# Token-shift mixing by token groups, each stored alone, and a shorter head before the mixing phase of a two-layer streaming trunk

## The chip, the cores and the metric

One core of a Trainium2 chip runs the whole program. Times are device microseconds (us) of one execution. The engines of the core run their own queues in the order fixed at build time: TensorE (PE in the profile, its weight loads PEld), VectorE (DVE), ScalarE (ACT), GpSimd (POOL) and SyncE (SP, which issues nearly all DMAs here). An instruction waits on semaphores for what other engines or transfers must have done.

## What is computed

Two layers of a streaming encoder. In each, one projection `w_in` of the normalised input feeds three parallel groups of heads: a short gated convolution, latent attention (MLA), and RWKV-7 time mixing. The time mixing works on columns that are first mixed with those of the token ahead. Cut to this part, the reference is:

```
h = rmsnorm(x, norm_g)
z = h @ w_in
xin, bg, cg, ga, cq, ckv, kr, gb, zc, gc = jnp.split(z, IN_OFFSETS, axis=-1)
...
prev = jnp.concatenate([shift_st[:, None].astype(zc.dtype), zc[:, :-1]], axis=1)
zs = zc + (prev - zc) * shift_mu
r, k, v, wl, al = jnp.split(zs, RWKV_OFFSETS, axis=-1)
...
ys, s_new = rwkv7_scan(r, decay, k, v, kk, a, wkv_st.astype(jnp.float32))
...
new_shift = zc[:, -1]
y = jnp.concatenate([y_a, y_b, y_c], axis=-1) @ w_out
return x + y, ckv_n, kr_r, new_conv, new_shift, s_new.astype(wkv_st.dtype)
```

Everything is float32. There are 1104 tokens: 64 of a running stream, 16 meta tokens, 1024 of a new stream.

## The kernel before

Columns lie on the 128 partitions, tokens along the free dimension. The tokens go in three groups, `GROUPS = ((0, 336), (336, 384), (720, 384))`; for the time mixing the 1104 tokens are padded to 1152 (`TP`), which are three groups of 384 (`GN`). `inproj` and `inproj_rest` project 24 tiles of 128 columns and the narrow tile `kr` (the keys' rotary part): per tile and group 24 matmuls, 8 blocks of the model width by three products of high and low halves in float32r (`hhi,whi`, `hlo,whi`, `hhi,wlo`); kr takes 16. In the profile all of these are `prj`. The halves of a weight are made on ScalarE (`whi`) and VectorE (`wlo`).

The seven columns of the time mixing come first, in the order `MIXED = (6, 2, 0, 4, 1, 3, 5)`. `part(m, g)` projects one group of column m and scales it out of PSUM into the tile `z`. When all three groups are there, `shifted(m)` mixes the column with the token ahead: GpSimd forms the difference of neighbours in a tile `zd` (1151 elements), VectorE writes the first tokens of both streams in it, and one `scalar_tensor_tensor` of VectorE over 1152 tokens adds `mu` times the difference to the column. SP then stores the whole column (576 KB) to an array in HBM, also named zd, and the set `have` gets m.

The time mixing itself is cut in six parts (a group of 384 tokens by a pair of heads). `prep` of a part waits until columns 6, p, 2+p and 4+p are in `have`, loads them from zd (`lora<-zd`, `wr<-zd`), and computes decays (`ldp`, `cum`), a first product X1 (`x`, masked on VectorE into `wq`), transpositions (`tm`), a triangular inverse in steps (`tri` by a round trip through HBM, then products `inv`) with a second product X2 (again `x`, masked into `wx`), and matrices `w`. `scan` then runs six steps of state products (`xp`, `sp`) and `finish` the outputs (`yp`, `ym`). Each part's prep may begin when the scan of the part ahead has begun.

`EARLY = 4` of the seven columns are projected before the phase `mix`. Inside `mix` the other projections are the main work, and after each matmul `pump` may issue pieces of the side streams (scan, finish, prep, and the preparation of the attention), when a planner (`Meter`), which keeps an estimated clock for each engine, holds that what they need is ready. When the projections are issued, `race` runs the attention and what is left of the side streams. The order so planned is then fixed per engine by the framework, which moves instructions by its own estimates.

Nearly all engine calls go through one recording helper, so the profile shows line 82 for them, and tiles tell them apart. A tile's number is left out in the profile's names.

Of the kernel before, what the change touches and what calls it, by code (L numbers as in the profile page):

```python
# [15 lines left out]
ALU = mybir.AluOpType  # L16
# [7 lines left out]
DEC = 64  # L24
# [5 lines left out]
TP = 1152  # L30
PAD0, PAD1 = DEC + NMETA, 128
GN = 384
GROUPS = ((0, 336), (336, 384), (720, 384))
# [18 lines left out]
ORDER = ("transpose", "outputs", "prepare", "scores")  # L52
KR = -1
MIXED = (6, 2, 0, 4, 1, 3, 5)
EARLY = 4
COLUMNS = (*(11 + m for m in MIXED), 18, 19, 0, 1, 2, KR, *range(3, 11), *range(20, 24))
NEVER = 1e9
LEAD = 0.0
# [8 lines left out]
P_NG, P_QG, P_KVG, P_MU, P_SH, P_A0, P_KK, P_KA, P_RK, P_LW, P_LB, P_CW, P_CS, P_FG, NPAR = (  # L67
    0, 8, 10, 11, 18, 25, 27, 29, 31, 33, 35, 37, 43, 47, 55)
# [127 lines left out]
class Net:  # L196
# [280 lines left out]
    def inproj(self, l, h, ms, begin=None, ready=None):  # L477

        nc, I, O = self.nc, self.I, self.O
        segs = lambda g: ((0, PAD0, 0), (PAD1, GN, PAD0)) if g == 0 else ((GN * g, GN * g + GN, 0),)  # L480
        if begin:
            self.sh = self.small("sh", [128, 7, 2], bufs=1)
        sh = self.sh
        w, xs = {}, {}

        def fetch(m):
            if m not in w:
                w[m], xs[m] = next(self.cols), self.S("tp", "z")
                nc.gpsimd.memset(xs[m][:, PAD0:PAD1], 0.0)

        def part(m, g):
            fetch(m)
            ps = self.project(w[m], h, g)
            if ready and m == ms[0]:
                ready(g)
            for b, e, s in segs(g):
                self.norm(xs[m][:, b:e], ps[:, s:s + e - b], g, s)

        def shifted(m):
            x, d = xs.pop(m), self.S("tp", "zd")  # L500
            nc.vector.tensor_copy(sh[:, m, 0:1], x[:, TP - 1:TP])
            nc.vector.tensor_copy(sh[:, m, 1:2], x[:, DEC - 1:DEC])
            nc.vector.tensor_copy(x[:, PAD1 - 1:PAD1], x[:, PAD0 - 1:PAD0])
            nc.gpsimd.tensor_tensor(out=d[:, 1:TP], in0=x[:, 0:TP - 1], in1=x[:, 1:TP], op=ALU.subtract)
            nc.vector.tensor_tensor(out=d[:, 0:1], in0=self.p(P_SH + m), in1=x[:, 0:1], op=ALU.subtract)
            nc.vector.tensor_scalar(d[:, DEC:DEC + 1], x[:, DEC:DEC + 1], -1.0, None, op0=ALU.mult)
            nc.vector.scalar_tensor_tensor(out=x, in0=d, scalar=self.p(P_MU + m), in1=x, op0=ALU.mult, op1=ALU.add)
            nc.gpsimd.memset(x[:, PAD0:PAD1], 0.0)
            nc.sync.dma_start(self.zd[m], x)
            self.have.add(m)  # L510

        first = FIRST if begin else 1
        for q in (ms[:first], *((m,) for m in ms[first:])):
            for g in range(3):
                if begin and q[0] == ms[0]:
                    begin(g, lambda g: fetch(q[0]))
                for m in q:
                    part(m, g)
            for m in q:
                shifted(m)  # L520
        if len(self.have) == 7:
            nc.sync.dma_start(O["shift"][l], sh)

    def gates(self, l, h, ms):
# [10 lines left out]
    def inproj_rest(self, l, h):  # L535
        nc, I, O = self.nc, self.I, self.O
        gs = list(enumerate(GROUPS))
        self.inproj(l, h, MIXED[EARLY:])
        yield
        yield from self.gates(l, h, (0, 1))  # L540

        cq = [self.S("z", "cq") for _ in range(2)]
# [1 line left out]
        for t, m in zip(cq + [ckv], range(3)):  # L544
            w = next(self.cols)
# [5 lines left out]
        for m in range(2):  # L551
            nc.vector.scalar_tensor_tensor(out=cq[m][:, :T], in0=cq[m][:, :T], scalar=self.p(P_QG + m),
                                           in1=rs[:, :T], op0=ALU.mult, op1=ALU.mult)
# [3 lines left out]
                                       op0=ALU.mult, op1=ALU.mult)  # L557
# [3 lines left out]
        w = next(self.cols)  # L561
# [343 lines left out]
    def rwkv(self, l):  # L905

        parts = [(g, hp) for hp in range(2) for g in range(3)]
        made, begun, done = {}, set(), {}

        def prep():  # L910
            for i, p in enumerate(parts):
                if i:
                    yield (lambda: i - 1 in begun,)
                yield (lambda: {6, p[1], 2 + p[1], 4 + p[1]} <= self.have,)
                yield from self.rwkv_prep(l, i, *p)
                made[i] = self.made
            self.prepped = True

        def scan():
            for i, p in enumerate(parts):  # L920
                yield (lambda: i in made,)
                begun.add(i)
                yield from self.rwkv_scan(l, i, *p, *made[i])
                done[i] = self.scanned

        def finish():
            for i, p in enumerate(parts):
                yield (lambda: i in done and ("gate", p[1]) in self.have,)
                yield from self.rwkv_finish(l, *p, *done[i])

        return [finish(), scan(), prep()]
# [460 lines left out]
    def run(self):  # L1392
# [33 lines left out]
        h = parts()  # L1426
        for l in range(self.depth):
# [12 lines left out]
                        self.sumsq(acc, x[k], k, GROUPS[g])  # L1440

            self.have = set()
            self.inproj(l, h, MIXED[:EARLY], begin, lambda g: self.inv(self.rs, acc, GROUPS[g]))
            self.mix(self.inproj_rest(l, h), self.rwkv(l), self.attention(l), self.outproj_first(l, xres))
            last = l == self.depth - 1
            if not last:
# [133 lines left out]
```

## Time and profile before

| | |
|---|---|
| three runs | 1526.41, 1530.67, 1530.34 us; median 1530.34 |
| the profiled execution's own time | 1529.08 us |
| its span, first to last instruction | 1527.0 us |
| mean granted TensorE clock | 0.988 of full speed |
| TensorE busy | 1463.1 us, 96% of the span |
| VectorE busy | 1063.0 us, 70% |
| ScalarE busy | 772.1 us, 51% |
| GpSimd busy | 253.1 us, 17% |
| projections of layer 0, with side streams | 82 to 443.4 us |
| projections of layer 1, with side streams | 818 to 1191.8 us |

Durations are those of one profiled execution, so sums are made against its own 1529.08 us. A row of a timeline gives the start, the duration, the engine, and in square brackets the time that the engine stood idle ahead of it and what ended that wait. Matmuls are pipelined: one starts about 0.17 us after the other though each lasts some 0.34, so what counts for TensorE is the distance of starts and the waits.

### The profile page before, as it was taken

Reading aid. Unit: us, or ns where it says so; the run is one execution under the profiler, and the core shown is the slowest. Engines: PE = TensorE matmul, PEld = TensorE weight load, DVE = VectorE, ACT = ScalarE, POOL = GpSimd, SP = SyncE. Lnnn points to the kernel's source line nnn. Section 1 sums busy time; section 2 is a strip of 40 time slices with the busy share of each in tenths; the row PEclk is TensorE's granted clock in tenths of the full one; section 3 lists DMA queues with packets and bytes.
Section 4 is the critical chain, followed back from the end, with each engine's and each line's share of the span. In section 5 each row is a group of like instructions: output and inputs, shape, how many; then the busy total and the mean of one; then the engine's idle time right before and its main releaser. Section 6 shows DMA issues by size and latency. Waiting matters only on the chain.

```text
span 1527.0 us, 30583 instructions
## 1 busy us (share of the span) xinstructions
PE 1463.1 (96%) x12076; PEld 1310.9 (86%) x12076; DVE 1063.0 (70%) x2477; ACT 772.1 (51%) x1846; POOL 253.1 (17%) x281
## 2 busy tenths in 40 slices
PE   8999999999999999999999999999999999999996
PEld 7989988999887878779999898898998768788795
DVE  7565687676778676575845666876767877686566
ACT  7125454444567575563522355445356775565442
POOL 0222212222121101000011222212122301111002
PEclk9999999999999999999999999999999999999998
DMA  6322212322225101122322312212322331012123
GB/s 209 137 83 81 68 50 57 88 55 75 82 86 164 31 26 39 55 74 63 141 103 99 117 33 60 88 30 81 76 67 77 129 98 47 24 35 85 41 66 119
DMA packets 95471, 119.81 MB, mean 78 GB/s; under 512 B 41889, under 2 KB 74785, under 8 KB 95329
## 3 DMA queue, kind: packets, MB, share of 16 engines
q1 hardware_dynamic: 95328, 117.87, 25.4%
q8 instruction: 95, 1.56, 0.4%
q14 instruction: 48, 0.39, 0.1%
HBM read 81.24 MB, written 36.60 MB: 77 GB/s over the span
## 4 chain that ended last, share of the span: by engine, by line
PE 51%; DVE 10%; ACT 5%; issue 3%; DMA 2%; POOL 1%; DVEq 0%; SPq 0%; ACTq 0%; POOLq 0%
PE prj L82 24%; PE sc L82 6%; PE po L82 6%; PE tr L82 5%; PE upq L82 3%; PE val L82 1%; PE inv L82 1%; DVE st L82 1%; DVE p L82 1%; PE upk L82 1%; ACT p L82 1%; DVE wq L82 1%; DVE out L82 1%; ACT pt L82 1%; ACT wq L82 1%
## 5 line engine op out<-in xcount | busy, mean ns | idle before, releaser
L82 PE MATMUL prj<-hhi,whi 128*128 128x384 f32 (+1 forms) x1152 | 392.0, 340 | 4.2 <-DVE z L82 2.6
L82 PE MATMUL prj<-hlo,whi 128*128 128x384 f32 (+1 forms) x1152 | 391.9, 340 | 0.1
L82 PE MATMUL prj<-hhi,wlo 128*128 128x384 f32 (+1 forms) x1152 | 391.1, 339 | 0.7 <-DVE wlo L82 0.7
L82 PEld LDWEIGHTS prj<-hhi,whi 128*128 128x128 f32 x1152 | 219.7, 191 | 7.5 <-issue 2.9
L82 PEld LDWEIGHTS prj<-hlo,whi 128*128 128x128 f32 x1152 | 219.6, 191 | 4.1 <-issue 0.9
L82 PEld LDWEIGHTS prj<-hhi,wlo 128*128 128x128 f32 x1152 | 219.5, 191 | 4.0 <-DVE wlo L82 1.0
L82 PE MATMUL prj<-yhi,wo 128*128 128x384 f32 (+2 forms) x776 | 206.5, 337 | 2.5 <-DVE xn L82 2.0
L82 PE MATMUL sc<-ka,qa 128*128 128x264 f32 (+9 forms) x720 | 156.3, 337 | 6.0 <-ACT p L82 2.5
L82 ACT ACTIVATE p<-sc,st 128x144 f32<-128x144 f32 (+8 forms) x240 | 127.9, 541 | 42.4 <-DVE st L82 41.6
L82 PEld LDWEIGHTS prj<-yhi,wo 128*128 128x128 f32 x776 | 138.6, 189 | 5.1 <-DVE xn L82 3.1
L82 DVE TENSOR_REDUCE st<-sc 128x1 f32<-128x512 f32 (+9 forms) x240 | 118.1, 501 | 23.9 <-PE sc L82 22.3
L82 PE MATMUL prj<-ylo,wo 128*128 128x384 f32 (+2 forms) x388 | 129.6, 334 | 0.0
L82 PEld LDWEIGHTS sc<-ka,qa 128*128 128x128 f32 (+1 forms) x720 | 112.3, 188 | 18.8 <-ACT p L82 6.4
L82 ACT ACTIVATE pt<-tr 128x512 f32<-128x512 f32 (+3 forms) x174 | 92.4, 546 | 70.2 <-PE tr L82 68.2
L82 PE MATMUL tr<-cst,p 128*128 128x128 f32 (+2 forms) x752 | 115.5, 277 | 4.5 <-ACT pt L82 3.1
L82 PEld LDWEIGHTS tr<-cst,p 128*128 128x128 f32 (+2 forms) x752 | 83.2, 141 | 28.3 <-issue 10.3
L82 POOL TENSOR_TENSOR qa<-qt,qa 128x512 fp32r<-128x512 f32 (+1 forms) x40 | 49.7, 1244 | 338.6 <-ACT qa L82 338.5
L82 ACT ACTIVATE whi<-wraw 128x1024 fp32r<-128x1024 f32 (+1 forms) x49 | 51.0, 1041 | 97.4 <-PE prj L82 82.5
L82 PE MATMUL po<-pt,v 128*64 128x256 f32 (+3 forms) x864 | 94.3, 354 | 0.4 <-ACT pt L82 0.4
L82 DVE TENSOR_SCALAR p<-p,st 80x336 f32<-80x336 f32 (+5 forms) x144 | 84.2, 587 | 1.8
L82 DVE TENSOR_TENSOR wlo<-wraw,whi 128x1024 fp32r<-128x1024 f32 (+1 forms) x49 | 71.4, 1458 | 16.9 <-ACT whi L82 16.8
L82 PEld LDWEIGHTS po<-pt,v 128*64 128x64 f32 (+1 forms) x864 | 53.2, 137 | 27.4 <-issue 4.5
(232 smaller groups left out, 2641.9 us busy)
## 6 DMA issues: line engine op xcount, KB each, us to landing
wraw<-w_in SPq DMA_DIRECT2D x47, 512.0 KB, 3.6
wraw<-w_out SPq DMA_DIRECT2D x32, 256.0 KB, 2.6
zd<-z SPq DMA_DIRECT2D x14, 576.0 KB, 3.5
wr<-zd SPq DMA_DIRECT2D x36, 192.0 KB, 2.8
gd<-gate SPq DMA_DIRECT2D x12, 552.0 KB, 3.4
yraw<-yd SPq DMA_DIRECT2D x8, 552.0 KB, 3.8
xn<-x SPq DMA_DIRECT2D x8, 552.0 KB, 4.2
xd<-xn SPq DMA_DIRECT2D x8, 552.0 KB, 2.9
```

Of the source, the lines that this page charges most:

```text
L82: r = f(*args, **kw)
```

## The change

Mixing goes by groups. `shifted(m, g)` is called after each group of a column: the difference covers the 383 elements inside the group, the first token of a group takes its neighbour from a copy of the last unmixed column of the group ahead (written into `d` at the next group's first place before that column is mixed), and the mix itself covers 384 tokens. Each group of a column is stored alone (192 KB), `have` holds pairs (column, group), and a part waits for the four pairs of its own group. `EARLY` is 3, so the projections of the fourth column are inside the phase `mix`, and `inproj` yields after each group, as the other projections do.

```diff
--- before.py
+++ after.py
@@ -52,7 +52,7 @@
 ORDER = ("transpose", "outputs", "prepare", "scores")
 KR = -1
 MIXED = (6, 2, 0, 4, 1, 3, 5)
-EARLY = 4
+EARLY = 3
 COLUMNS = (*(11 + m for m in MIXED), 18, 19, 0, 1, 2, KR, *range(3, 11), *range(20, 24))
 NEVER = 1e9
 LEAD = 0.0
@@ -481,7 +481,7 @@
         if begin:
             self.sh = self.small("sh", [128, 7, 2], bufs=1)
         sh = self.sh
-        w, xs = {}, {}
+        w, xs, ds = {}, {}, {}
 
         def fetch(m):
             if m not in w:
@@ -496,18 +496,28 @@
             for b, e, s in segs(g):
                 self.norm(xs[m][:, b:e], ps[:, s:s + e - b], g, s)
 
-        def shifted(m):
-            x, d = xs.pop(m), self.S("tp", "zd")
-            nc.vector.tensor_copy(sh[:, m, 0:1], x[:, TP - 1:TP])
-            nc.vector.tensor_copy(sh[:, m, 1:2], x[:, DEC - 1:DEC])
-            nc.vector.tensor_copy(x[:, PAD1 - 1:PAD1], x[:, PAD0 - 1:PAD0])
-            nc.gpsimd.tensor_tensor(out=d[:, 1:TP], in0=x[:, 0:TP - 1], in1=x[:, 1:TP], op=ALU.subtract)
-            nc.vector.tensor_tensor(out=d[:, 0:1], in0=self.p(P_SH + m), in1=x[:, 0:1], op=ALU.subtract)
-            nc.vector.tensor_scalar(d[:, DEC:DEC + 1], x[:, DEC:DEC + 1], -1.0, None, op0=ALU.mult)
-            nc.vector.scalar_tensor_tensor(out=x, in0=d, scalar=self.p(P_MU + m), in1=x, op0=ALU.mult, op1=ALU.add)
-            nc.gpsimd.memset(x[:, PAD0:PAD1], 0.0)
-            nc.sync.dma_start(self.zd[m], x)
-            self.have.add(m)
+        def shifted(m, g):
+
+            x, b, e = xs[m], GN * g, GN * g + GN
+            if g == 0:
+                ds[m] = self.S("tp", "zd")
+            d = ds[m]
+            if g == 0:
+                nc.vector.tensor_copy(sh[:, m, 1:2], x[:, DEC - 1:DEC])
+                nc.vector.tensor_copy(x[:, PAD1 - 1:PAD1], x[:, PAD0 - 1:PAD0])
+            if g == 2:
+                nc.vector.tensor_copy(sh[:, m, 0:1], x[:, TP - 1:TP])
+            else:
+                nc.vector.tensor_copy(d[:, e:e + 1], x[:, e - 1:e])
+            nc.gpsimd.tensor_tensor(out=d[:, b + 1:e], in0=x[:, b:e - 1], in1=x[:, b + 1:e], op=ALU.subtract)
+            nc.vector.tensor_tensor(out=d[:, b:b + 1], in0=d[:, b:b + 1] if g else self.p(P_SH + m), in1=x[:, b:b + 1], op=ALU.subtract)
+            if g == 0:
+                nc.vector.tensor_scalar(d[:, DEC:DEC + 1], x[:, DEC:DEC + 1], -1.0, None, op0=ALU.mult)
+            nc.vector.scalar_tensor_tensor(out=x[:, b:e], in0=d[:, b:e], scalar=self.p(P_MU + m), in1=x[:, b:e], op0=ALU.mult, op1=ALU.add)
+            if g == 0:
+                nc.gpsimd.memset(x[:, PAD0:PAD1], 0.0)
+            nc.sync.dma_start(self.zd[m, :, b:e], x[:, b:e])
+            self.have.add((m, g))
 
         first = FIRST if begin else 1
         for q in (ms[:first], *((m,) for m in ms[first:])):
@@ -516,9 +526,9 @@
                     begin(g, lambda g: fetch(q[0]))
                 for m in q:
                     part(m, g)
-            for m in q:
-                shifted(m)
-        if len(self.have) == 7:
+                    shifted(m, g)
+                yield
+        if len(self.have) == 21:
             nc.sync.dma_start(O["shift"][l], sh)
 
     def gates(self, l, h, ms):
@@ -535,8 +545,7 @@
     def inproj_rest(self, l, h):
         nc, I, O = self.nc, self.I, self.O
         gs = list(enumerate(GROUPS))
-        self.inproj(l, h, MIXED[EARLY:])
-        yield
+        yield from self.inproj(l, h, MIXED[EARLY:])
         yield from self.gates(l, h, (0, 1))
 
         cq = [self.S("z", "cq") for _ in range(2)]
@@ -911,7 +920,7 @@
             for i, p in enumerate(parts):
                 if i:
                     yield (lambda: i - 1 in begun,)
-                yield (lambda: {6, p[1], 2 + p[1], 4 + p[1]} <= self.have,)
+                yield (lambda: {(m, p[0]) for m in (6, p[1], 2 + p[1], 4 + p[1])} <= self.have,)
                 yield from self.rwkv_prep(l, i, *p)
                 made[i] = self.made
             self.prepped = True
@@ -1440,7 +1449,8 @@
                         self.sumsq(acc, x[k], k, GROUPS[g])
 
             self.have = set()
-            self.inproj(l, h, MIXED[:EARLY], begin, lambda g: self.inv(self.rs, acc, GROUPS[g]))
+            for _ in self.inproj(l, h, MIXED[:EARLY], begin, lambda g: self.inv(self.rs, acc, GROUPS[g])):
+                pass
             self.mix(self.inproj_rest(l, h), self.rwkv(l), self.attention(l), self.outproj_first(l, xres))
             last = l == self.depth - 1
             if not last:
```

In what follows the order of instructions on one engine is shown before and after the change. First VectorE in layer 0, where the first part's X1 product (`x`) is masked into `wq`: `z<-prj,rs` scales a projection out of PSUM, `zd` and `z<-zd,par,z` are the mixing, `sh` keeps a stream's last column. Before:

```order
L82 TENSOR_TENSOR z_796<-prj_873,rs_167 128x384
L82 TENSOR_TENSOR wlo_932<-wraw_794,whi_931 128x1024
L82 COPY sh_168<-z_796 128x1
L82 TENSOR_SCALAR zd_921<-z_796 128x1
L82 SCALAR_TENSOR_TENSOR z_796<-zd_921,par_88,z_796 128x1152
L82 TENSOR_TENSOR wq_840<-x_128_963,cst 128x384
L82 TENSOR_TENSOR wq_840<-x_129_964,cst 128x384
```

The same place now:

```order
L82 TENSOR_TENSOR z_868<-prj_918,rs_167 128x384
L82 TENSOR_TENSOR wx_891<-wr_669,wa_830 128x3x2x64
L82 SCALAR_TENSOR_TENSOR wr_669<-wr_669,par_88 128x384
L82 COPY zd_908<-z_868 128x1
L82 TENSOR_TENSOR zd_908<-zd_908,z_868 128x1
L82 SCALAR_TENSOR_TENSOR z_868<-zd_908,par_88,z_868 128x384
L82 TENSOR_TENSOR wq_831<-x_123_981,cst 128x384
L82 TENSOR_TENSOR wq_831<-x_124_982,cst 128x384
```

Ahead of the masks there stands the mix of one group in place of that of a whole column.

Next VectorE in layer 0 among the rows of kr: `kr` and `krt` are its rotation and its low halves, `wr<-xp` belongs to a scan step, `wlo` is a weight's low half, `u` and `lora` are small rows of the convolution and of the next part. Before:

```order
L82 COPY tri_2207<-tri_2207 48x256
L82 TENSOR_TENSOR kr_2305<-kr_2305 32x384
L82 SCALAR_TENSOR_TENSOR kr_2305<-krt_2306,rot 32x384
L82 TENSOR_TENSOR wlo_2394<-wraw_2303,whi_2393 128x1024
L82 SCALAR_TENSOR_TENSOR krt_2306<-krt_2306,rot 32x384
L82 TENSOR_TENSOR wr_1412<-xp_2425,wq_1423 64x128
L82 TENSOR_TENSOR kr_2305<-kr_2305,krt_2306 32x384
```

The last rows of kr now, and what follows them:

```order
L82 SCALAR_TENSOR_TENSOR kr_2390<-krt_2391,rot 32x384
L82 TENSOR_TENSOR wlo_2477<-wraw_2388,whi_2476 128x1024
L82 SCALAR_TENSOR_TENSOR krt_2391<-krt_2391,rot 32x384
L82 TENSOR_TENSOR kr_2390<-kr_2390 32x384
L82 TENSOR_TENSOR kr_2390<-kr_2390,krt_2391 32x384
L82 COPY u_2474<-par_88 128x2
L82 MEMSET u_2474 128x2
L82 TENSOR_SCALAR lora_2763<-lora_2763 64x384
L82 TENSOR_TENSOR kr_2390<-kr_2390 32x384
L82 TENSOR_TENSOR wx_2114<-x_318_2531,cst 128x384
L82 TENSOR_TENSOR wx_2114<-x_319_2532,cst 128x384
```

The scan row is gone from here (part 1's scan is over before kr), the tri rows stand ahead of kr, and the masks of part 2's X2 product stand behind kr's last low half.

On TensorE the first products of part 2's inverse stood 79 to 81 projections after kr's last one. Before:

```order
L82 MATMUL prj_2504<-hlo_161,whi_2393 128x336
L82 MATMUL prj_2504<-hhi_153,wlo_2394 128x336
L82 MATMUL yp_2572<-wr_1412,wq_1423 64x64 x6
L82 MATMUL inv_2542<-wq_2054,wa_2053 64x64 x12
L82 MATMUL inv_2555<-wa_2053,wq_2054 64x64 x12
```

Now the second product comes 31 projections after kr's end, behind the X2 product (`x_318`, `x_319`) and outputs of part 1 (`yp`):

```order
L82 MATMUL x_318_2531<-wb_2112,wx_2114 64x128
L82 MATMUL x_319_2532<-wb_2112,wx_2114 64x128
L82 MATMUL yp_2546<-wr_1440,wq_1451 64x64 x12
L82 MATMUL inv_2569<-wq_2063,wa_2062 64x64 x12
L82 MATMUL inv_2582<-wa_2062,wq_2063 64x64 x12
L82 MATMUL prj_2510<-hlo_161,whi_2384 128x384
```

It moved 50 projections towards kr. On the whole VectorE has 86 rows more, GpSimd and SP 28 each; TensorE's instructions are the same in number. The first `ldp` stands 356 projections into layer 0 where it stood 397. At the end of a layer's projections three xp and four sp were still to be issued before; now one sp.

## Rows read from the trace of the kernel before

**Rows 1.** Busy times by stretch, layer 0's projections (columns as in the head line)
```profile
core 0: us, PE busy (x) PEld busy (x) DVE busy (x) ACT busy (x) POOL busy (x), PEclk, DMA share, GB/s
82.00:443.40 361.40, 347.33 (x3424) 321.12 (x3423) 252.06 (x556) 178.57 (x400) 79.75 (x90) 0.99 0.25 70
```
**Rows 2.** Waits of TensorE, 82 to 443 us (waited for: us in total, times, longest)
```profile
PE sp L82 <- ACT wx L82: 4.0, 2, 3.7
PE inv L82 <- DVE wx L82: 3.2, 3, 1.4
PE tm L82 <- ACT wa L82: 2.1, 1, 2.1
...
PE w L82 <- DVE wq L82: 0.8, 1, 0.8
```
**Rows 3.** Waits of TensorE, 818 to 1192 us
```profile
PE sp L82 <- ACT wx L82: 3.9, 2, 3.6
...
PE tm L82 <- ACT wa L82: 2.0, 1, 2.0
...
PE inv L82 <- DVE wa L82: 1.2, 1, 1.2
```
**Rows 4.** Timeline of TensorE, 95 to 98.3 us: last projection, and tm
```profile
95.75 0.33 PE L82 MATMUL prj<-hhi,whi 128*128 128x384 f32 x1
98.17 0.33 PE L82 MATMUL tm<-cst,wx 128*128 128x128 f32 x1 [2.09 <-ACT wa L82]
```
**Rows 5.** Timeline of VectorE, 93 to 98.2 us
```profile
95.61 0.15 DVE L82 TENSOR_SCALAR zd<-z 128x1 f32<-128x1 f32 x1 [1.94 <-POOL zd L82]
95.80 1.42 DVE L82 SCALAR_TENSOR_TENSOR z<-zd,par,z 128x1152 f32<-128x1152 f32 x1
97.14 1.02 DVE L82 TENSOR_TENSOR wq<-x,cst 128x384 f32<-128x384 f32 x2
```
**Rows 6.** Timeline of GpSimd, 92 to 96 us
```profile
92.62 2.96 POOL L82 TENSOR_TENSOR zd<-z 128x1151 f32<-128x1151 f32 x1 [4.98 <-issue]
```
**Rows 7.** Timeline of TensorE, 228 to 233 us
```profile
228.19 0.33 PE L82 MATMUL prj<-hlo,whi 128*128 128x384 f32 x1
228.36 0.34 PE L82 MATMUL prj<-hhi,wlo 128*128 128x384 f32 x1
232.35 0.80 PE L82 MATMUL sp<-wr,wt 128*128 128x128 f32 x2 [3.65 <-ACT wx L82]
```
**Rows 8.** Timeline of VectorE, 213 to 236 us: the rows of kr and between
```profile
214.44 0.50 DVE L82 TENSOR_TENSOR krt<-prj,krt 64x336 f32<-64x336 f32 x1
...
226.42 0.36 DVE L82 COPY tri<-tri 48x256 f32<-48x256 f32 x1
...
228.11 1.15 DVE L82 SCALAR_TENSOR_TENSOR kr<-krt,rot 32x384 f32<-32x384 f32 x1
229.29 1.81 DVE L82 TENSOR_TENSOR wlo<-wraw,whi 128x1024 fp32r<-128x1024 f32 x1
...
231.71 0.28 DVE L82 TENSOR_TENSOR wr<-xp,wq 64x128 f32<-64x128 f32 x1
...
233.64 1.38 DVE L82 TENSOR_TENSOR kr<-kr 32x384 fp32r<-32x384 f32 x1
```
**Rows 9.** DMA issues: KB each, median us from issue to landing
```profile
zd<-z SPq DMA_DIRECT2D x14, 576.0 KB, 3.5
```
**Rows 10.** Timeline of TensorE, 238 to 243 us: part 2's inverse
```profile
239.26 0.85 PE L82 MATMUL inv<-wa 64*64 64x64 f32 x21
...
240.77 0.42 PE L82 MATMUL prj<-hlo,whi 128*128 128x336 f32 x1
241.03 0.32 PE L82 MATMUL prj<-hhi,wlo 128*128 128x336 f32 x1
...
241.68 0.84 PE L82 MATMUL inv<-wq,wa 64*64 64x64 f32 x22
```
**Rows 11.** Timeline of VectorE, 205 to 211.5 us: part 2's reduction, first tri row
```profile
205.79 0.79 DVE L82 TENSOR_REDUCE dg<-wq 128x96 f32<-128x384 f32 x1
...
210.75 0.15 DVE L82 TENSOR_TENSOR lora<-tri 48x12 f32<-48x12 f32 x1
```
**Rows 12.** Waits of TensorE, 1191.8 to 1440 us
```profile
PE sp L82 <- ACT wx L82: 0.5, 1, 0.5
```

## The prediction

> **What bounds the kernel now.** I read the busy shares by stage first: while the projections of a layer run, TensorE is busy 347 of 361 us in layer 0, and VectorE only 252 of them, 70% [rows 1]; layer 1 looks the same. So a microsecond can be won or lost only in the 14 us per layer in which TensorE stands still, or by giving it more work. Of the profiled execution's 1529.08 us (span 1527.0) nothing else is touched; the median of the three runs is 1530.34, so 1.26 goes on top of a sum against the former. "0.3%" below is 4.6 us, about what a measurement of this kernel can tell from no change.
>
> Next I read what TensorE waited for in those stages. In both layers the largest entries are the state products of a scan (sp, 4.0 and 3.9 us), three products of the triangular inverse (inv), and one wait of a transposition (tm, 2.1 and 2.0 us) [rows 2, 3]. Then, for each, the timeline at its place, on TensorE and on the engine that came late.
>
> The tm wait is at 95.75 to 98.17: tm stood 2.09 us, put down to ACT wa [rows 4]. ACT there copies the same PSUM tiles that VectorE masks, and VectorE was late: it stood 1.94 us for GpSimd's difference of a whole column, then mixed 1152 tokens in 1.42 us, and only then, at 97.14, masked the tiles [rows 5]. GpSimd's difference took 2.96 us [rows 6].
>
> The sp wait is in the projection of the key columns kr: sp stood 3.65 us until 232.35 [rows 7]. VectorE had a queue of kr rows; the row that sp needs, wr<-xp, came to run at 231.71, behind a product of 1.15 us and a weight half of 1.81 [rows 8], with a third low half still to come. No gap of VectorE stands in between: it was a backlog.
>
> **The change part by part.** *The mix by groups.* Per column GpSimd's one difference becomes three, VectorE's six rows become twelve, SP's one store becomes three; two layers have 14 columns: 86 rows more on VectorE, 28 on each of the others. VectorE: a 384-wide row takes 0.51 us (two masks in 1.02 [rows 5]), so three mixes are 1.5 us for 1.42, and four to six tiny rows of 0.15 at overlapped starts come on top: about 0.6 us per column, 4 us per layer. I cost it at nothing: VectorE has 109 us idle in that stage [rows 1]; if the cover went it would cost these 4 us per layer. GpSimd: 80 of 361 us busy [rows 1], the differences keep their elements; nothing.
> The Trainium skill speaks against the split (VectorE: DVE Perf Modes, section on the TRN2 errata): each instruction that reads SBUF pays a fixed extra latency, so many small tiles pay it often. The rows agree in direction (1.5 for 1.42), but by either the extra lies on an engine with 30% to spare.
> The stores: 576 KB landed in 3.5 us [rows 9]; a third of it lands no later. What waits for it is a part's loads, which now need small stores rather than large ones, so they can only come earlier, on no path of TensorE, and the DMA share is 0.25 in the stage [rows 1]. Twenty-eight more issues on SP: nothing, no TensorE wait names them.
> The Trainium skill (DMA: Bandwidth & Descriptors, section on the anatomy of one DMA) gives every transfer a fixed cost of about 2 us; 28 of them would be 56 us if somebody stood behind each, and by the rows nobody does.
>
> *The tm wait.* The rows behind it become a 384-token mix, and the X1 product now has eight instead of five projections between it and its transposition in layer 0. VectorE can still be held by a third of GpSimd's difference, about 1 us, which eight projections at 0.17 us cover. I take the wait as gone in both layers: −2.09 − 2.0 = **−4.1**. Bounds: 0 to −4.1.
>
> *Parts start earlier.* A part asks for its own group, and three columns rather than four stand before the mixing: the first ldp comes 41 projections earlier. All parts shift, so that at kr other rows meet. Scan 1 is over before kr in the new order: both sp waits of 3.6 go. But part 2's second inverse now comes 31 projections after kr's 48. Its PSUM tile is freed by the two X2 masks on VectorE, and these stand behind the kr rows. Call kr's first projection T. TensorE gets there at 79 × 0.17 = 13.4 us, plus the first inverse and the X2 product, 2.4 us from 239.26 to 241.68 [rows 10]: T + 15.8. VectorE: the X1 product of part 2 ends about 13 us before T (34 projections, 6 us; scan, transposition and sum-of-squares instructions, 7 us). Masks and reduction take 2.2 us, the round trip to the first tri row 4.2 (reduction ending at 206.58, tri at 210.75 [rows 11]), the 17 tri rows 6.2 and the scan and weight rows between them 3.6, the two cq rows 2.7: −13 + 2.2 + 4.2 + 9.8 + 2.7 is T + 5.9, so the kr rows begin near T + 6. Before, kr's rows reached from 214.44 to the end of the last low half at 235.02, 20.6 us [rows 8]; out of that go 13 tri rows (the last at 226.42) and three scan rows, 6.5 us, and two diagonal rows, the ckv row and the X2 masks come in, 3.5 us: 17.6 us, end T + 23.6. That is 7.8 us too late. If the six kr, lora and weight rows that took 1.15 to 1.81 beside GpSimd ran unhindered, 4.1 us less: 3.7 us too late. I take 5.0 us in layer 0, nearer to the lower end, since consecutive rows of VectorE overlap by some 0.08 us, which these sums leave out for the rows that come in, and 4.5 in layer 1, where one low half stands behind the masks. Net of what goes: 5.0 + 4.5 − 3.65 − 3.56 = **+2.3**; bounds −7.2 to +8.4.
>
> *The ends of the stages.* Before, three xp and four sp of the last part run after the projections, in each layer; now one sp. There sp waited 0.5 us in layer 1 [rows 12], and I take 0.4 for layer 0 by that row: **−0.9**. The steps of the last part are set closer for it: from its last inverse to w 1.8 us instead of 2.9, where w already waited 0.8 [rows 2]. I take half of the 1.1 us per layer: **+1.0** (0 to 2.2).
>
> *TensorE's own work.* The same instructions; switches between float32 and float32r runs rise by 12, that is six round trips. The first projection after such a run took 0.26 us to the next, from 240.77 to 241.03 [rows 10], against 0.15 among projections of 336 columns, 0.11 more each: **+0.7**.
>
> **The sum**: −4.1 + 2.3 − 0.9 + 1.0 + 0.7 = −1.0, so 1528.1 against the profiled execution, 1529.3 against the median.
>
> **The rivals.** *A, faster: VectorE catches up at kr.* If tri, scan and cq rows end some 5 us earlier than I have them, no wait replaces sp's 7.2 us: −7.2 in place of +2.3, sum −10.5, 1519.8. For it: the X1 product of part 2 moves ahead by 34 projections, and VectorE is 30% idle. Against: VectorE had no gap from 214 to 235, and no kr row goes away.
> *B, slower: the backlog at kr is the whole of it.* At before's hindered durations the second inverse waits 7.8 us, and the third, a few projections later in layer 1, stands behind the same rows for another 1.2, as long as one inv waited for DVE wa in layer 1 [rows 3]: 9.0 per layer, net +10.8 for +2.3, sum +7.5, 1537.8. The point from which it decides: above 5.3 us per layer the change is slower than before, above 7.6 by over 0.3%. For it: GpSimd is as busy beside kr as before. Against: those rows lay beside one another by chance of the order, which is new.
> *C, the wait moves only from whole columns to groups.* VectorE stands for each of three differences, and the tm wait stays: +4.1 on my sum, 1533.4. Against: 1 us pieces and eight projections of cover.
> That the change does not do what it says is excluded by the order: stores, differences and starts are where the diff puts them.
>
> **How the numbers follow.** My forecast 0.50, A 0.20, B 0.17, C 0.13. The forecast's own bounds (3.7 to 7.8 us at kr, tm −4.1 to −2, w 0 to 2.2) give 1525.5 to 1536, mostly within 4.6 us of before. The range reaches from A, 1519.5, to nearly B, 1536.5, and leaves out half of A and half of B. Faster by over 0.3%: A and a seventh of the forecast, 0.27. Slower: most of B, a little of C and the forecast, 0.19. Within: 0.54.
>
> **What would show it.** Right: no tm wait over 0.5 us at the first X1 masks; the sp waits at kr gone, and an inv wait of 4 to 6 us on DVE wx some 15 to 20 us after kr's start in both layers; the last part over a few microseconds after the projections end. A: no wait over 2 us around kr. B: one over 7.5. C: 2 us of tm again, with GpSimd's zd as what VectorE waited for. Wrong altogether: a new wait of over 2 us outside these places, such as a part's ldp or lora load behind its stores, or projections waiting for weights at the start of a layer.

## The result, and the profile after

The changed kernel is slower: 1541.53 us (median of 6 runs) against 1530.51, a ratio of 1.0072 (95% interval 1.0055 to 1.0089). The forecast was 1529.3, within 0.3% of before, with 1536.5 as the upper end.

The page of the kernel after, span and busy times:

```profile
span 1538.3 us, 30765 instructions
## 1 busy us (share of the span) xinstructions
PE 1461.3 (95%) x12076; PEld 1311.0 (85%) x12076; DVE 1081.5 (70%) x2570; ACT 768.6 (50%) x1837; POOL 269.9 (18%) x309
```

The span grew by 11.3 us. TensorE is busy 1.8 us less than before, so all of it is waiting. (Work that runs at a lower clock counts as busy; the last section comes back to this.) I added up every entry of TensorE's waits, by stretch:

| stretch | before, us | after, us |
|---|---|---|
| start, to 82 us | 6.2 | 7.4 |
| layer 0's projections up to kr | 4.0 | 4.0 |
| at kr (to 246 us) | 3.7 | 6.5 |
| from there to the last projection | 6.0 | 9.8 |
| attention and output of layer 0 | 6.6 | 7.9 |
| layer 1's projections up to kr | 4.0 | 2.5 |
| at kr | 3.6 | 4.5 |
| from there to the last projection | 6.3 | 10.6 |
| attention, output, end | 11.1 | 12.1 |

That is 51.5 against 65.3 us. The larger part does not lie at kr, where the prediction looked, but behind it. TensorE's waits after, layer 0's projections (82 to 454 us; total, times, longest):

```profile
PE inv L82 <- DVE wx L82: 9.3, 3, 6.5
PE sp L82 <- ACT wx L82: 4.7, 5, 2.2
PE inv L82 <- DVE wq L82: 2.3, 1, 2.3
...
PE w L82 <- DVE wq L82: 1.4, 1, 1.4
```

and layer 1's (820 to 1206 us):

```profile
PE inv L82 <- DVE wx L82: 6.6, 2, 4.5
PE sp L82 <- ACT wx L82: 3.8, 3, 2.0
PE inv L82 <- DVE wq L82: 2.2, 1, 2.2
PE w L82 <- DVE wq L82: 1.9, 2, 1.4
PE tm L82 <- ACT wa L82: 1.6, 1, 1.6
```

Against [rows 2, 3]: sp's 3.6 us at kr and the first part's tm waits (2.1 and 2.0 us) are gone in both layers. The 1.6 us of tm in layer 1 is another one, at 948.78 us, in the preparation of part 2. Beside it four kinds of wait are new. The first stands at kr, as forecast. TensorE's timeline after, 226 to 238 us:

```profile
226.79 0.63 PE L82 MATMUL yp<-wr,wq 64*64 64x64 f32 x15
233.95 1.55 PE L82 MATMUL inv<-wq,wa 64*64 64x64 f32 x24 [6.53 <-DVE wx L82]
...
237.51 0.52 PE L82 MATMUL prj<-hhi,whi 128*128 128x384 f32 x1
237.83 0.52 PE L82 MATMUL prj<-hlo,whi 128*128 128x384 f32 x1
```

VectorE's timeline after, the rows of kr and the masks:

```profile
216.80 0.50 DVE L82 TENSOR_TENSOR krt<-prj,krt 64x336 f32<-64x336 f32 x1
218.32 0.50 DVE L82 SCALAR_TENSOR_TENSOR kr<-krt,rot 32x336 f32<-32x336 f32 x1 [1.02 <-POOL krt L82]
...
232.66 0.55 DVE L82 TENSOR_TENSOR kr<-kr 32x384 fp32r<-32x384 f32 x1 [0.24 <-ACT kr L82]
233.24 1.02 DVE L82 TENSOR_TENSOR wx<-x,cst 128x384 f32<-128x384 f32 x2
```

With T for the start of kr's first projection, 211.05 us, VectorE's first row of kr is at T + 5.8 and the masks end at T + 23.2 (forecast T + 6 and T + 23.6). TensorE stood there from T + 16.4 (forecast T + 15.8).

The second new wait is sp's 2.2 us at 162.38 (2.0 at 1037 in layer 1). The rows at it, in order, of VectorE, SP, ScalarE and TensorE:

```profile
157.94 0.54 DVE L82 COPY tri<-tri 48x256 f32<-48x256 f32 x1
...
157.98 0.32 SPq L82 DMA_DIRECT2D lora<-zd  x1
...
160.40 1.63 ACT L82 ACTIVATE lora<-lora 64x384 f32<-64x384 f32 x3 [3.26 <-DMA lora<-zd]
162.05 0.27 ACT L82 ACTIVATE wx<-xp 64x128 f32<-64x128 f32 x1
...
162.38 0.49 PE L82 MATMUL sp<-wr,wt 128*128 128x128 f32 x2 [2.21 <-ACT wx L82]
```

The triangular work of one part uses the lora tile as its scratch. The next part's load into that tile is issued when this work ends, and ScalarE, which has the next part's three rows ahead of the scan's wx, stands for the load.

The third and fourth are the last part's inverse and w. VectorE and TensorE after, 403 to 423 us:

```profile
403.77 1.20 DVE L82 CAST kc<-kr 32x256 fp32r<-32x256 f32 x2
...
406.80 0.62 DVE L82 CAST ka<-kr 32x384 fp32r<-32x384 f32 x2
407.45 1.02 DVE L82 TENSOR_TENSOR wx<-x,cst 128x384 f32<-128x384 f32 x2
...
408.94 0.92 PE L82 MATMUL inv<-wq,wa 64*64 64x64 f32 x24 [2.30 <-DVE wq L82]
...
419.76 2.47 DVE L82 CAST ka<-kr 32x336 fp32r<-32x336 f32 x6 [2.87 <-POOL wq L82]
422.26 0.35 DVE L82 COPY wq<-inv 32x192 f32<-32x192 f32 x1
```

The casts copy the rotated keys for the attention (`attn_shared`). They stand, with a state row and a gate row, ahead of the masks that free the PSUM tile. Six more of them, which VectorE began only after standing 2.87 us for GpSimd, are ahead of the copy into wq that w waits 1.40 us for.

### The profile page after: what moved, and what is told of

Same layout as the page of the kernel before. It is cut to its first block, busy times and chain, and to the rows that moved or that the text cites. A ratio compares the mean times of both kernels' runs of the same rounds, so it can differ in the third digit from the quotient of the medians.

```text
span 1538.3 us, 30765 instructions
## 1 busy us (share of the span) xinstructions
PE 1461.3 (95%) x12076; PEld 1311.0 (85%) x12076; DVE 1081.5 (70%) x2570; ACT 768.6 (50%) x1837; POOL 269.9 (18%) x309
## 5 line engine op out<-in xcount | busy, mean ns | idle before, releaser
L82 PE MATMUL sc<-ka,qa 128*128 128x144 f32 (+8 forms) x720 | 155.0, 336 | 2.7 <-ACT p L82 1.8
L82 DVE TENSOR_REDUCE st<-sc 128x1 f32<-128x512 f32 (+8 forms) x240 | 117.7, 503 | 20.7 <-PE sc L82 18.4
L82 PEld LDWEIGHTS prj<-ylo,wo 128*128 128x128 f32 x388 | 73.1, 188 | 0.2
```

Of the source, the lines that this page charges most:

```text
L82: r = f(*args, **kw)
```

## The experiments

Ratios are to the kernel before, run on the same chip, with the 95% interval.

**Theory A**: the loss comes from where steps of the parts meet other rows in VectorE's and ScalarE's queues. **Theory B**: the mixing by groups costs by itself. **Theory C**: projecting the fourth column inside the phase `mix` costs by itself.

**e1**, the kernel before with
```diff
-EARLY = 4
+EARLY = 3
```


> The kernel before with EARLY = 3 alone: columns are mixed and stored whole, and a part waits for whole columns. By the order the first three parts stand where they stood before and the last three are set closer, as in the change (first inverse of the last part after 1605 projections instead of 1660). Theory A (the loss comes from where the parts' steps now stand: the second inverse behind the kr rows of VectorE, and closer steps of the last parts): tm's 2.1 us and sp's 3.6 us at kr stay, the last three parts wait some 4 us more per layer, of which the shorter race gives back about 2: 1532 to 1536 us, a third of the change's loss. Theory B (mixing by groups costs by itself, through its extra instructions on VectorE, GpSimd and SP): none of that is here, so no difference, 1529 to 1532. Theory C (projecting the fourth column inside the phase is what costs): nearly the whole loss, 1538 to 1542.

Measured: 1520.94 us, 0.9934 (0.9912 to 0.9955), faster, which none of the three expected. Theory C falls. tm's 2.1 and sp's 3.7 us stayed. From layer 0's last projection to layer 1's first it took 310.6 us instead of 318.4, and 5.1 less from layer 1's last projection to the last of the output: the last three scan steps of each layer's last part no longer stand between the attention's work. The projections, which now carry these steps, took 5.7 us more in layer 0 and 3.9 in layer 1. That makes the profiled span 3.6 us shorter; TensorE's waits add up to 51.1 us, as before. The profiled execution is the slowest of e1's six, and where the rest of the 10 us comes from is not shown. This part of the change is a gain, so if the parts of the change add up, the rest lost more than the 11 us that show.

**e2**, the change with `EARLY = 4`.

> The change with EARLY back at 4. By the order layer 0 stands as before (the group waits move nothing there, first ldp at 402 projections instead of 397), with the mixing by groups in it; in layer 1 the first three parts move as in the change (part 2's second inverse 31 projections after kr), and the last three are spaced as before. So layer 0 shows the cost of the mixing itself and layer 1 that of the collision at kr. Theory A: layer 0 loses tm's wait or less, no inv wait over 2 us at kr, and 3.6 us of sp at kr; layer 1 has an inv wait of 4 to 5 us at kr: 1530 to 1534 us. Theory B: nearly all of the loss is here, 1537 to 1541, with layer 0 some 4 to 5 us longer than before without one large wait. Theory C: no loss, 1528 to 1531.

Measured: 1536.39 us, 1.0026 (1.0012 to 1.0041), above A's 1530 to 1534 and below B's. The layers differ as A says: in layer 0 the tm wait is gone and kr begins 2.3 us earlier than before, with sp's 3.68 us at kr as before; layer 1 has 6.55 us of inv at kr and 2.3 of sp behind a lora load, and its projections took 12.2 us more than before.

**e3**, the change with part waits for whole columns:
```diff
-                yield (lambda: {(m, p[0]) for m in (6, p[1], 2 + p[1], 4 + p[1])} <= self.have,)
+                yield (lambda: {(m, g) for m in (6, p[1], 2 + p[1], 4 + p[1]) for g in range(3)} <= self.have,)
```


> The change, but a part waits for whole columns. By the order layer 0 has the first three parts where they stood before and the last three closer; layer 1 stands as layer 0 of the change, with the collision at kr. Theory A: layer 0 keeps sp's 3.6 us at kr and has the closer steps' 4 us; layer 1 has an inv wait of 4 to 7 us at kr and the closer steps: 1534 to 1539 us. Theory B: as the change, 1539 to 1543. Theory C: as the change, 1539 to 1543.

Measured: 1534.06 us, 1.0017 (1.0004 to 1.0031), at A's lower end. Both layers mix by groups, but only layer 1's first three parts stand where the change has them. Waits of e3, 82 to 443.5 us (layer 0):

```profile
PE sp L82 <- ACT wx L82: 5.2, 3, 3.7
...
PE inv L82 <- DVE wx L82: 2.4, 2, 1.4
```

and 793 to 1197 us (layer 1):

```profile
PE inv L82 <- DVE wx L82: 9.9, 3, 6.6
PE sp L82 <- ACT wx L82: 5.0, 5, 2.2
PE inv L82 <- DVE wq L82: 2.2, 1, 2.2
```

e3 differs from e1 in the mixing by groups alone and is 13 us slower, which looks like theory B. But layer 0, with the same mixing, has none of the new waits, and its projections were done 5.5 us earlier than e1's; it is layer 1, where the parts moved with the mixing, whose projections took 441.9 us for e1's 433.5, with the waits above. So the rows of the mixing cost nothing by themselves, and theory B falls.

**e4**, the change with part 2's inverse held until the first tile after kr is projected:
```diff
-        yield Q, Tm, kt, "rw+", "next"
+        yield Q, Tm, kt, "rw+", "next", (lambda: i != 2 or self.past_kr)
...
+            self.past_kr = True
             w = next(self.cols)
             nc.vector.tensor_copy(u[:, 0:2], self.p(P_CS + 2 * m, 2))
...
```


> The change with one condition more: the inverse of part 2 may be issued only when the first tile after kr (its three groups, 72 projections) has been projected. By the order its second inverse then stands 73 projections after kr instead of 31, about 7 us later, and the parts behind it move later with it (first inverse of the last part after 1658 projections instead of 1596). Theory A: the inv waits of 6.5 and 4.5 us at kr fall to under 2 us, with the slow clock behind them, no sp wait comes back there, and the last parts wait less: 1526 to 1532 us, most of the loss gone or better than before. Theories B and C: the work that waits is only pushed, or the loss lies elsewhere: 1536 to 1541.

Measured: 1517.07 us, 0.9903 (0.9883 to 0.9923): 24 us less than the change. In layer 0 the wait at kr is 1.46 us. Waits add up to 47.3 us instead of 65.3, and TensorE's busy time fell by 4.9 us (last section). But the hold moves all parts behind it too, the last one by 50 to 60 projections.

**e5**, the hold moved to the tile's second group:
```diff
+                self.past_kr = self.past_kr or g == 1
                 yield
```


> As e4, but the inverse of part 2 is held only until two groups of the first tile after kr are projected. By the order VectorE's rows at kr and the two masks behind them stand exactly as in the change, the second inverse comes 18 projections later in layer 0 and 35 later in layer 1, and the last three parts stand where the change has them (first inverses after 1174, 1382 and 1596 projections, in the change 1165, 1382 and 1596). So the collision at kr is the only thing that is much changed. Theory A (VectorE's queue at kr makes the wait, and the slow clock behind a long wait adds to it): 18 projections are 3.2 us, so layer 0's wait falls from 6.5 to 3.4 us; layer 1's, 4.5 us, goes. With a third to a half of that again for the clock: 8 to 12 us less than the change, 1530 to 1534 us. Rival (the closer steps of the last parts make the loss, and holding part 2 helped in e4 by spreading them): no more than 2 us less, 1538 to 1542. Rival (an inverse that is held longer waits the less for some other reason, such as the transfers of tri): the wait falls in neither layer by the 18 and 35 projections.

Measured: 1535.98 us, 1.0023 (1.0015 to 1.0032), 5.5 us less than the change, where A expected 8 to 12. TensorE in e5 at kr, layer 0:

```profile
232.59 0.69 PE L82 MATMUL inv<-wq,wa 64*64 64x64 f32 x8 [3.58 <-DVE wx L82]
```

Layer 0's wait fell as computed (3.4); layer 1's fell by half, to 2.3 us, where it was to go. New waits came up in part 2's and 3's scans: xp 2.3 us for VectorE's state, sp 3.2 us with ScalarE standing 5.8 us for a lora load. The last part, which had not moved, waited 2.1 and 1.4 us as in the change.

**e6**, the change with kr's low halves left out (ScalarE writes zeros):
```diff
-        self.halves(*self.krs[0], krc)
+        self.high(*self.krs[0], krc)
```
and so for the three groups of kr.

> The change without the low halves of the rotated keys: VectorE's four subtractions at kr are left out, and ScalarE writes zeros there (four more copies on ScalarE), so this part of the scores has the precision of the high halves alone. The masks then stand behind four rows less on VectorE in layer 0 (1.13, 1.19, 1.14 and 0.55 us in the change's trace), and TensorE's order at kr is that of the change. Theory A: the inv wait at kr falls from 6.5 to some 2.5 us in layer 0 and from 4.5 to about 1 in layer 1; with the clock 8 to 12 us less than the change, 1530 to 1535 us. Rival (the wait belongs to the tri round trip or to the POOL products of kr, and VectorE's rows lie beside it): the waits stay over 5 and 3.5 us, 1538 to 1542.

Measured: 1548.18 us, 1.0094 (1.0079 to 1.0110), slower than the change: a miss. The wait at kr in layer 0 fell from 6.5 to 4.8 us only. VectorE, with four rows less, stood three times for GpSimd's product of kr (2.8 us), where it stood once (1.0) in the change. One of these rows, and the masks, on VectorE, and two rows of ScalarE in e6:

```profile
227.70 1.23 DVE L82 SCALAR_TENSOR_TENSOR kr<-krt,rot 32x384 f32<-32x384 f32 x1 [0.90 <-POOL krt L82]
...
231.06 1.00 DVE L82 TENSOR_TENSOR wx<-x,cst 128x384 f32<-128x384 f32 x2
...
231.17 1.05 ACT L82 ACTIVATE kr<-kr 32x384 fp32r<-32x384 f32 x2 [3.93 <-DVE kr L82]
232.24 0.49 ACT L82 ACTIVATE wa<-inv 128x384 f32<-128x384 f32 x1
```

The masks end 20.4 us behind kr's start instead of 23.2, so leaving out the low halves brought them 2.8 us forward. The inverse began 0.7 us behind the masks all the same: TensorE's wait ended with ScalarE's `wa`, which stood behind a kr copy that this experiment added. So e6 does not isolate the low halves, and how much of the 4.8 us is the chain through GpSimd is not shown. And the next part, moved a little, met the lora load: ScalarE in e6, with a weight half queued behind it that VectorE and then the inverse needed (4.75 us of inv at 292.29):

```profile
288.31 0.52 ACT L82 ACTIVATE lora<-lora 64x384 f32<-64x384 f32 x1 [12.78 <-DMA lora<-zd]
288.74 1.04 ACT L82 ACTIVATE whi<-wraw 128x1024 fp32r<-128x1024 f32 x1
```

**e7**, e4 with `EARLY = 4`.

> e4 with EARLY = 4: in layer 0 the order is that of the kernel before but for the mixing by groups, in layer 1 the collision is held off. Theory A, with e1's finding (EARLY = 3 alone gave 10 us, since six scan steps of the last part leave the attention's phase in each layer): e2 less the 9 to 11 us of its collision in layer 1, 1525 to 1528 us, so 8 to 11 us slower than e4. If EARLY does nothing by itself beside the hold: as e4, 1515 to 1519.

Measured: 1532.81 us, 0.9998 (0.9985 to 1.0011), slower than its 1525 to 1528, 16 us behind e4. So EARLY = 3 is worth at least as much beside the hold as without it (10 us in e1), and layer 1's hold gave back 3.6 us of e2's loss, not 9 to 11: the wait at kr there fell from 6.55 to 3.24 us.

**e8**, e4 with the scratch in another tile than lora:
```diff
-        flat, room = tri.rearrange("p i r k -> p (i r k)"), room[:48]
+        flat, room = tri.rearrange("p i r k -> p (i r k)"), self.tmp("cube")[:48]
```


> e4 with the scratch of the triangular work in another tile than the one that the next part's lora load goes to. In the change and in e4 that load is issued only when the triangular work of the part ahead has ended, and ScalarE, waiting for it, holds up the scan's wx: an sp wait of 2.2 us in layer 0 (159.8 us in the change) and of 2.0 in layer 1. By the order parts 3 to 5 move as well. If the buffer is the cause, the sp wait with ScalarE's lora in front of it goes: 1512 to 1517 us. If the load waits for something else: the wait stays, 1516 to 1520.

Measured: 1512.19 us, 0.9869 (0.9848 to 0.9890), the fastest version, 20 us below the kernel before. ScalarE's waits for lora fell from 38.5 us in e4 to 7.0, and no sp wait behind one is left. Parts 3 to 5 moved as well, so the 5 us are not the buffer's alone.

**e9**, the same edit on the kernel before.

> The kernel before with the scratch of the triangular work in another tile than lora, nothing else; TensorE's order is the same row for row. ScalarE then no longer stands for the lora loads (38 us before), but TensorE's waits of before name lora at no place: they are tm's 2.1, sp's 3.6 at kr, inv's. Theory (the late lora load hurts only where parts follow each other closely, as in the change): at most 3 us gained, 1529 to 1533. Rival (the late load is a cost of its own in every order, of the 5 us that e8 gained on e4 or more): 1523 to 1528.

Measured: 1533.41 us, 1.0007 (0.9995 to 1.0020): nothing. **e12**, the same on e1:

> e1 (whole columns, EARLY = 3) with the scratch moved; TensorE's order as in e1. tm's and sp's waits stay; e1 has an sp wait of 1.3 us in the fourth part of each layer. By e9's theory 1 to 4 us faster than e1, 1517 to 1521 us; if moving the scratch is worth 5 us anywhere, 1514 to 1517.

Measured: 1519.98 us, 0.9932 (0.9919 to 0.9945), as e1. The late load costs nothing by itself in these two orders; that it costs where a scan step is queued behind it is what the rows of the change (sp at 162.38) and e8 say.

**e10**, the same on the change, no hold.

> The change with the scratch moved, no hold. The planner now puts part 2 earlier: by the order its second inverse stands at the 39th of kr's 48 projections instead of 31 behind them, and VectorE's X2 masks stand in front of the cq, ckv and kr rows instead of behind; a scan row of part 2 (wr from xp) is now the one behind kr's last low halves. Theory A (what is queued behind kr's rows on VectorE waits): the inv waits of 6.5 and 4.5 us at kr go, an sp wait of 3 to 4 us comes back there as in the kernel before, and the sp waits of 2.2 and 2.0 us behind lora go: 1522 to 1530 us. Rival (the loss is the closer spacing of all parts, which is the same or closer here: first inverse of the last part after 1587 projections, in the change 1596): 1538 to 1543.

Measured: 1534.45 us, 1.0031 (1.0015 to 1.0047): it gives back 7 of the change's 11 us, less than A expected. Layer 0's inv wait at kr and the sp waits behind lora went, but sp waited 4.6 us at 280 for a row of VectorE that stood behind the round trip of tri, and 3.1 at 1151.

**e11**, e8 with waits for whole columns.

> e8, but a part waits for whole columns. By the order layer 0 has the first three parts where they stood before (with sp's 3.6 us at kr, without tm's wait) and layer 1 nearly as e8. If e8's gain needs the parts to start by groups: 3 to 6 us slower than e8, 1516 to 1519 us. If the earlier start gives nothing by itself: as e8, 1510 to 1515.

Measured: 1516.83 us, 0.9905 (0.9889 to 0.9921), 5 us behind e8. That the start by groups is worth this much is not shown: the intervals touch (e8 up to 0.9890), and the profiled executions have the same waits, 44.4 us here and 44.8 in e8. What e11 does show is that mixing by groups, with the hold, is no slower than the whole columns of e12.

**e13**, the change with the last part's inverse held until the fourth gate column:
```diff
-        yield Q, Tm, kt, "rw+", "next"
+        yield Q, Tm, kt, "rw+", "next", (lambda: i != 5 or self.past_gate)
...
             self.have.add(("gate", m))
+            self.past_gate = m >= 3
...
```


> The change with the inverse of the last part alone held until the fourth gate column is projected: by the order it stands after 1633 projections instead of 1596, and every part ahead of it, with the collision at kr, stands as in the change. In the change's trace this inverse waits 2.3 and 2.2 us for VectorE, whose masks stand between copies of the keys for the attention (kc and ka from kr) that the end of the last part's preparation sets free, w waits 1.4 us in each layer, and the attention's first queries and transpositions wait 1.1 and 1.5 us. Theory A (each wait is a meeting of a part's step with other rows of VectorE at that place): the inv and w waits of the last part change by more than 1.5 us per layer, while the waits at kr, 6.5 and 4.5, stay; 1534 to 1539 us if they fall, and as the change or slower if the new place is no better. Rival (the closer spacing of the last parts is what costs): 37 projections more of room take most of the 8 us that the trace shows behind kr, 1531 to 1535.

Measured: 1530.26 us, 0.9995 (0.9982 to 1.0007): the 11 us of the change, with the collision at kr untouched. Waits of e13, 82 to 452 us:

```profile
PE inv L82 <- DVE wx L82: 10.5, 4, 6.6
PE sp L82 <- ACT wx L82: 4.7, 5, 2.2
...
PE w L82 <- DVE wq L82: 1.0, 1, 1.0
```

The inv wait on DVE wq is gone (2.3 and 2.2 us). The time is below what A expected and even below the rival's 1531 to 1535. The profiled span fell by 7.2 us: some 5 us of waits, of which only 1.3 and 0.7 lie between kr and the last projection, and 2.5 us of TensorE's busy time. The rest of the 11 is the choice of the profiled execution, the slowest of twelve here and a faster one than the median in the change. So the last part's place is shown to cost about as much as the whole loss; that it is the casts alone, and not the closer spacing, is not.

**e14**, e8 with that hold.

> e8 with the last part's inverse held in the same way: layer 0's moves from 1605 to 1633 projections, layer 1's stands at 1643 already. If the later place is better for the last part: 1 to 3 us faster than e8, 1509 to 1511. If layer 0's place was good: as e8 or up to 3 us slower, 1512 to 1515.

Measured: 1516.97 us, 0.9915 (0.9899 to 0.9932), 5 us slower than e8, above both expectations. So the later place is not better everywhere. That speaks for the place and against the spacing, with few runs (five and six) that overlap.

## Why the prediction was wrong

**The mixing at nothing: right.** Layer 0 of e2 and e3 has it without a loss.

**tm gone, −4.1: right.** In layer 0 kr began 2.3 and 2.5 us earlier in e2 and e3; in layer 1 too the first part's tm came without a wait (0.03 us, at 843), but part 2's waited 1.6 us, at a place that the prediction did not look at.

**The net at kr, +2.3: right in kind, a little small.** The queue at hindered durations was computed within half a microsecond (T + 23.2 for T + 23.6). The discount from 7.8 to 5.0 us, for rows that would run unhindered, was too large in layer 0: four kr rows there still took 1.13 to 1.19 us each. The waits were 6.5 and 4.5 us for 5.0 and 4.5, net +3.7. That they are queue waits is shown by e5 in layer 0 (3.2 us later, 2.95 us less).

**The failed step** is the one on the ends of the stages, with its sentence "I take half of the 1.1 us per layer: +1.0 (0 to 2.2)". It took a later part's cost to be w's room alone and every other step of the moved parts to be neutral. w did grow, by 0.6 and 0.6 us per longest wait. But the waits behind kr grew by 3.8 and 4.3 us, with the inverse of the last part (2.3, 2.2) queued behind casts that were named nowhere, and by 2.3 more in the attention and the end, where the prediction had −0.9. e13 moved that part alone and had the loss back in time, though only 2.0 us of these waits behind kr went with it.

**A term was missing**: the next part's lora load, 2.2 and 2.0 us of sp, which the prediction named only as a sign of being wrong altogether. The text followed the stores (no wait of TensorE names them) and not the tile that the load goes into; e9 and e12 show that it costs nothing in the orders with whole columns.

**A gain was missed too**: EARLY = 3 gives 10 us alone (e1), where the prediction had −0.9 for the scan steps out of the attention and +1.0 for the closer steps, together +0.1.

**TensorE's own work, +0.7**, does not show: its busy time fell by 1.8 us.

**The range** was too narrow by the prediction's own terms: the upper bounds of 7.8 us twice at kr, −2 for tm and 2.2 for w add up to 1538.7, not 1536. The measured time lies above that too.

**The rivals.** B, the backlog at kr at 1537.8, came nearest in time, for a reason that held about a quarter of the new waits: +3.7 of the 13.8 us. Above 5.3 us per layer at kr the change was to be slower than before; the two waits average 5.5, which by the prediction's sum is only half a microsecond slower. C did not happen in either layer.

What stays open: how the loss divides among the places. The holds do not add up (e5 gives 5.5, e13 11, e4 24 us, and each moves what lies behind it), and e13 gained more than its trace's waits. A hold on the kernel before, which would tell whether holding a part is a gain of its own, was not run.

## What to carry to other kernels

When a change makes a stream start earlier, its price need not lie at the place one looks at first: list every later step that moves, and read for each what now stands ahead of it in the queue of the engine that releases it, on VectorE and ScalarE alike. A step held back by some forty projections gave back as much as the change had lost (e13) or more (e4), and groups, holds and a free scratch tile together were the fastest here (e8). Split a change that does two things: one half of this one was a gain of 0.66% (e1).

## What the runs showed of the hardware that was not expected

TensorE's clock fell during a long wait, and the work that had waited then ran at the lower level. The stretches of the kernel after around kr (time, PE, PEld, DVE, ACT, POOL busy, granted clock, DMA share, GB/s):

```profile
229.00:233.00 4.00, 0.00 (x0) 0.00 (x0) 3.67 (x8) 0.52 (x1) 2.01 (x2) 0.56 0.50 139
233.00:240.00 7.00, 6.05 (x59) 5.96 (x60) 5.03 (x11) 1.03 (x3) 0.00 (x0) 0.52 0.16 37
240.00:246.00 6.00, 6.00 (x100) 5.64 (x98) 0.34 (x1) 1.49 (x3) 3.42 (x4) 1.00 0.03 10
```

After 6.5 us of standing, the clock was at its lower level, 1.2 GHz, until some 6 us into the work (the first two stretches show 0.56 and 0.52, the third 1.00): projections started 0.32 us apart in place of 0.17 (the rows of 237.51 and 237.83), and a run of 24 inv matmuls lasted 1.55 us, where 22 took 0.84 before [rows 10]. The kernel before shows the like behind sp's 3.6 us (0.54 of full speed from 232 to 239 us), so it does not part the two at kr; but it puts a further price on a wait of that size that a change adds.

This price is not in the sums of waits, and it differs between executions. Behind sp's wait of 2.2 us at 162 us the clock of the stretch from 160 to 165 us was 1.00 in the change and 0.72 in e13, where the wait was the same. Over whole executions the time goes with the mean granted clock: the five of e8 lie between 1508.01 us at 0.996 and 1518.92 at 0.988. The versions differ as much: the median clock was 0.984 in the change, 0.988 in e13 and 0.993 in e4. e4's profiled span is 23.0 us shorter than the change's, of which 18.0 are waits and 4.9 TensorE's busy time, with the same number of instructions. So e4 and e13 gained more than their waits. It is no rule of this record: the change waits longer than the kernel before and its busy time is 1.8 us shorter.
